# A two-layer attention, retention and convolution network on one core: buffers on multiples of 64 bytes, weights that start some words behind one, a new first phase and split retention values

## The chip, the core and the metric

The kernel runs on one core of one Trainium2 chip. The metric is the device time of one execution in microseconds; before the change it was 2833.11 (median of two runs, 2832.78 and 2833.45). The core has a matrix engine (TensorE, PE in the profile; PEld is its loading of the stationary operand), VectorE (DVE), ScalarE (ACT), GpSimd (POOL) and SyncE (SP, which issues most transfers). The engines run side by side, each through its own list of instructions in order, and wait for each other by semaphores. SBUF is the working memory, 128 partitions wide; a product of TensorE is summed up in a PSUM bank and emptied from there by ScalarE or VectorE.

## The reference

One sequence of 256 tokens, 2048 features, two layers. All weights and activations are float32.

```python
for l in range(DEPTH):                       # 2
    hn = _rmsnorm(h, norm_mix[l])
    if l % 2 == 0:
        h = h + _mixer_ab(hn, ...)           # 8 MoBA heads and 8 NSA heads, 2048 x 5400 in, 2048 x 2048 out
    else:
        h = h + _mixer_c(hn, ...)            # 8 retention heads, 2048 x 12288 in, 4096 x 2048 out
    h = h + _cross_attn(_rmsnorm(h, norm_cross[l]), mem_n, w_q_x[l], w_kv_x[l], w_o_x[l])
    h = h + _conv_ffn(_rmsnorm(h, norm_ffn[l]), w_up[l], conv_w[l], conv_b[l], w_down[l])   # d_ff 5632
return _rmsnorm(h, norm_final)
```

In retention each head has queries and keys of 256, values of 512, and chunks of 128 tokens; in a chunk the output is `(q k^T * decay) v`, and across chunks a decayed state is carried. The values are centred later by a group norm over 512 features.

## The kernel before

Activations are held with features on partitions, in 16 slabs (`xs`, 32 buffers of 512 words): columns 0 to 255 are the activation rounded to float32r (`xhat_hi`, L197, ScalarE), columns 256 to 511 what the rounding left (`xhat_lo`, L200, VectorE). float32r is a 4-byte type that keeps fewer bits of the fraction. Weights come from HBM in pieces of 1024 words a partition (`raw`, 4 buffers) and are split in the same way: `whi` by ScalarE (L232), `wlo` by VectorE (L233), 4 buffers of each, so that splitting can run four pieces ahead of TensorE. Three products, high by high, high by low and low by high, then make one product of almost full float32 precision.

There are two forms. `product_b_steps` has the weights stationary (128 of them at a time) and the slabs moving: L272 sends 512 columns (the high weights against both halves), L277 sends 256 (the low weights against the high half). `product_a_steps` has the activations stationary and the weights moving, 512 wide as a rule, 256 or 280 in the first stage (L307 to L309). One product of the first form takes 32 instructions of L272 and 32 of L277. Attention and retention inside a head use full float32 (L975 to L988 in retention), which TensorE runs in two passes an instruction.

The order on TensorE is the order of the code (`manual_schedule`). Work beside the products, such as a head's attention, stands in generators on a list `side`; after every step of a product `pump` moves the first two on that list forward by one `yield`. So a count of `yield`s fixes how many products lie between two parts of a head. The order on ScalarE and VectorE is set by the framework's scheduler, apart from the first phase, which is written out by hand for ScalarE, VectorE and TensorE.

The first phase (L378 to L414) makes two products at once, the columns 4096 to 4607 of `w_in_ab`, while x and weights come in: it loads `mix` gains, then two slabs of x (L373) and 512 words of both weight pieces (L393) at a time, makes the slab's halves (L197, L200), the weights' halves (L406, L401, L407), and sends the products for two slabs. Its four accumulators are all that there are, so the first `product_a` waits until `halves` (L326, L328) has emptied two of them. `start_steps` (L624) is on `side` then: it loads the rows of x a second time, as tokens on partitions, in eight parts (L376), sums their squares on ScalarE (`norm.add`, L148) and makes the norm's factor `col`, `row` and what hangs on it, the angles of the rotation (`angle_steps`) included.

In retention (`head` in `mixer_c`) the values are scaled by the norm's factor on the way out of PSUM with their sum taken along (L963), then shifted by their mean (L965). `attend` makes `q k^T` (L975, L977), multiplies it by the decay (L979, L980), and two `yield`s later multiplies by the values in float32 (L986, L988).

SBUF buffers lie behind each other, each starting on a multiple of 32 bytes. A few small ones (4 to 128 bytes) come first, and by them all `xs`, `raw`, `whi` and `wlo` buffers start 32 bytes behind a multiple of 64 in the built program.

Of the kernel before, what the change touches and what calls it, by code (L numbers as in the profile page):

```python
# [75 lines left out]
def hybrid_kernel(ctx: ExitStack, tc: tile.TileContext, a, out):  # L76
# [5 lines left out]
    count = [0]  # L82
# [12 lines left out]
    def small(n):  # L95
        return new([P, n], F32, "small", 12)
# [13 lines left out]

    ident = new([P, P])
    make_identity(nc, ident)
    ones = new([P, P])
    pool.memset(ones, 1.0)
# [98 lines left out]


# [150 lines left out]
    SPANS = [range(k, k + 2) for k in range(0, ND, 2)]  # L365
# [5 lines left out]
    def load_x(p):  # L371

        nc.sync.dma_start(x_in[p].rearrange("p s t -> p (s t)"), a["x"][:, 2 * p * S : (2 * p + 2) * S])  # L373
# [5 lines left out]
    with tc.manual_schedule(engines=engines):  # L379
        act.activation(new([P, 1]), eps, AF.Copy, scale=eps)  # L380
        load_par(nc.sync, "mix")
        for p in range(ND // 2):
            i, c = p // 2, slice(p % 2 * 512, p % 2 * 512 + 512)
            if p % 2 == 0:
                raws = [raw_tile() for _ in range(2)]
                his = [new([P, 1024], F32R, "whi", 4) for _ in range(2)]
                los = [new([P, 1024], F32R, "wlo", 4) for _ in range(2)]
            if p < 4:
                load_x(p)
            for q in range(2):  # L390
                if p < 4 or p % 2 == 0:
                    d = c if p < 4 else slice(0, 1024)
                    nc.sync.dma_start(raws[q][:, d], w_ab.part(4 * i, 4, 4096 + 256 * q, 256)[:, d])  # L393
            if p == 3:
                for x in range(4, 8):
                    load_x(x)
            for s in (2 * p, 2 * p + 1):
                xs_mix.append(slab_tile())
                xhat_hi(xs_mix[s], x_in[p][:, s % 2, :], gain("mix")[:, s : s + 1])
            if p == 0:  # L400
                dve.tensor_copy(his[0][:, c], raws[0][:, c])  # L401
            for s in (2 * p, 2 * p + 1):
                xhat_lo(xs_mix[s], x_in[p][:, s % 2, :], gain("mix")[:, s : s + 1])
            for q in range(2):
                if p or q:
                    act.activation(his[q][:, c], raws[q][:, c], AF.Copy)  # L406
# [806 lines left out]
```

## Time and profile before

| | |
|---|---|
| median of two runs | 2833.11 us |
| profiled execution, its own time | 2834.51 us |
| its span, first to last instruction | 2832.8 us |
| TensorE busy | 2812.4 us (99%), 14726 instructions |
| VectorE busy | 1906.3 us (67%) |
| ScalarE busy | 1460.1 us (52%) |
| mean granted TensorE clock | 0.998 |
| transferred | 530.11 MB, 187 GB/s over the span |

The profile gives busy time per engine and per group of instructions with their mean length, what ended the idle time before them, and the chain of work that ended last. A product's length in the groups (391 ns for a 512-wide one) includes its way through the array, which the next product's overlaps; the step from one start to the next, or a stretch of the chain divided by its count, is the time that it costs.

### The profile page before, as it was taken

How to read it: one execution, taken by the hardware profiler on the slowest of the kernel's cores; microseconds unless marked ns; L12 is line 12 of the kernel's file. 1: busy time of each engine (PE TensorE's matmuls, PEld its weight loads, DVE VectorE, ACT ScalarE, POOL GpSimd, SP SyncE). 2: the span in 40 equal slices, each digit the busy share in tenths (PEclk: the TensorE clock that was granted, in tenths of full speed). 3: DMA queues.
4: the chain of work that ended last, by engine and by line, in shares of the span. 5: the costliest groups of instructions: out<-in, count | busy, mean ns of one | idle time of the engine just before them, and what ended most of it. 6: DMA issues, size and time to landing. Idle time of an engine off the chain costs nothing.

```text
span 2832.8 us, 39488 instructions
## 1 busy us (share of the span) xinstructions
PE 2812.4 (99%) x14726; PEld 2406.5 (85%) x14726; DVE 1906.3 (67%) x3147; ACT 1460.1 (52%) x2193; POOL 29.9 (1%) x211
## 2 busy tenths in 40 slices
PE   8999999999999999999999999999999999999998
PEld 7888888888888888888888888888888888888887
DVE  7765776776767677665555555556767767676766
ACT  6454455654545455454444444444665645454544
POOL 0000000000000000000000000000000000000000
PEclk9999999999999999999999999999999999999999
DMA  8535565455555555555555555555545555555554
GB/s 305 171 126 161 180 211 172 170 189 192 187 198 190 189 196 201 194 179 179 179 178 186 193 178 179 182 206 189 189 164 193 186 196 184 193 193 187 197 186 158
DMA packets 150544, 530.11 MB, mean 187 GB/s; under 512 B 17040, under 2 KB 17456, under 8 KB 150352
## 3 DMA queue, kind: packets, MB, share of 16 engines
q1 hardware_dynamic: 148752, 523.65, 54.7%
q0 software_dynamic: 1024, 2.90, 0.3%
q8 instruction: 115, 1.88, 0.3%
q10 hardware_dynamic: 576, 1.05, 0.1%
q14 instruction: 77, 0.63, 0.1%
HBM read 525.43 MB, written 2.10 MB: 186 GB/s over the span
## 4 chain that ended last, share of the span: by engine, by line
PE 98%; DMA 1%; ACT 0%; DVE 0%; SPq 0%; issue 0%; ACTq 0%; DVEq 0%
PE acc L272 32%; PE acc L277 17%; PE acc L307 14%; PE acc L309 14%; PE acc L308 14%; PE bank L350 1%; PE bank L986 0%; DMA t<-in_w_in_ab_dram 0%; PE bank L504 0%; PE bank L496 0%; PE bank L484 0%; DMA t<-in_rows_dram 0%; PE bank L1009 0%; PE bank L589 0%; PE bank L579 0%; PE bank L975 0%
## 5 line engine op out<-in xcount | busy, mean ns | idle before, releaser
L233 DVE TENSOR_TENSOR t<-t,t 128x1024 fp32r<-128x1024 f32 x954 | 1156.6, 1220 | 568.7 <-ACT t L232 522.9
L232 ACT ACTIVATE t<-t 128x1024 fp32r<-128x1024 f32 x954 | 1004.6, 1057 | 739.6 <-PE acc L309 540.6
L272 PE MATMUL acc<-t,t 128*128 128x512 f32 x4096 | 965.9, 391 | 6.2 <-DVE t L200 6.2
L272 PEld LDWEIGHTS acc<-t,t 128*128 128x128 f32 x4096 | 759.7, 188 | 159.1 <-DVE t L200 6.2
L307 PE MATMUL acc<-t,t 128*128 128x512 f32 (+2 forms) x1824 | 713.3, 391 | 4.9 <-DVE t L328 4.9
L309 PE MATMUL acc<-t,t 128*128 128x512 f32 (+2 forms) x1824 | 705.1, 387 | 0.0
L308 PE MATMUL acc<-t,t 128*128 128x512 f32 (+2 forms) x1824 | 704.5, 386 | 0.0
L277 PEld LDWEIGHTS acc<-t,t 128*128 128x128 f32 x4096 | 510.6, 192 | 11.6 <-issue 0.4
L277 PE MATMUL acc<-t,t 128*128 128x256 f32 x4096 | 518.0, 283 | 0.0
L307 PEld LDWEIGHTS acc<-t,t 128*128 128x128 f32 x1824 | 343.9, 189 | 74.7 <-DVE t L328 5.4
L309 PEld LDWEIGHTS acc<-t,t 128*128 128x128 f32 x1824 | 343.6, 188 | 69.5
L308 PEld LDWEIGHTS acc<-t,t 128*128 128x128 f32 x1824 | 343.9, 189 | 68.9 <-issue 1.9
L883 ACT ACTIVATE t<-acc 128x256 f32<-128x256 f32 x176 | 65.8, 374 | 229.6 <-PE acc L272 229.6
L886 DVE TENSOR_TENSOR t<-acc,t 128x256 f32<-128x256 f32 x176 | 74.1, 421 | 157.2 <-ACT t L883 157.2
L889 ACT ACTIVATE t<-t,t 128x256 f32<-128x256 f32 x176 | 103.8, 590 | 1.1
L210 ACT ACTIVATE t<-t 128x256 fp32r<-128x256 f32 x88 | 36.1, 411 | 130.5 <-DVE t L908 130.5
L607 DVE TENSOR_TENSOR t<-t,acc 128x512 f32<-128x512 f32 x148 | 95.1, 680 | 2.8 <-PE acc L1104 2.8
L891 DVE SCALAR_TENSOR_TENSOR t<-t,t,t 128x256 f32<-128x256 f32 x176 | 84.2, 478 | 1.5
L890 DVE SCALAR_TENSOR_TENSOR t<-t,t,t 128x256 f32<-128x256 f32 x176 | 84.2, 478 | 0.2
L326 ACT ACTIVATE t<-acc 128x256 f32<-128x256 f32 x80 | 30.0, 376 | 103.4 <-PE acc L272 103.4
L328 DVE TENSOR_TENSOR t<-acc,t 128x256 f32<-128x256 f32 x80 | 33.4, 419 | 69.7 <-ACT t L326 69.7
L887 DVE TENSOR_TENSOR t<-t,t 128x256 f32<-128x256 f32 x176 | 74.3, 422 | 3.0
(218 smaller groups left out, 1127.6 us busy)
## 6 DMA issues: line engine op xcount, KB each, us to landing
t<-in_w_up_dram SPq DMA_DIRECT2D x352, 512.0 KB, 3.4
t<-in_w_in_c_dram SPq DMA_DIRECT2D x192, 512.0 KB, 3.5
t<-in_w_down_dram SPq DMA_DIRECT2D x176, 512.0 KB, 3.4
t<-in_w_in_ab_dram SPq DMA_DIRECT2D x80, 512.0 KB, 4.2
t<-in_w_out_c_dram SPq DMA_DIRECT2D x64, 512.0 KB, 3.3
t<-in_w_out_ab_dram SPq DMA_DIRECT2D x32, 512.0 KB, 4.2
t<-in_w_kv_x_dram SPq DMA_DIRECT2D x32, 512.0 KB, 3.8
t<-in_w_q_x_dram SPq DMA_DIRECT2D x16, 512.0 KB, 3.2
```

The source lines that it names most:

```text
L232: act.activation(hi[:, 0 : m * ncol], raw[:, 0 : m * ncol], AF.Copy)
L233: dve.tensor_sub(lo[:, 0 : m * ncol], raw[:, 0 : m * ncol], hi[:, 0 : m * ncol].bitcast(F32))
L272: pe.matmul(acc[j], parts[k - k0][0][:, j * P : (j + 1) * P], xs[k], start=(k == 0), stop=(end and k == n - 1))
L277: pe.matmul(acc[j][:, 0:S], parts[k - k0][1][:, j * P : (j + 1) * P], xs[k][:, 0:S], start=False, stop=(end and k == n - 1))
L307: pe.matmul(o, xh, hi, start=(k == 0), stop=False)
L308: pe.matmul(o, xh, lo, start=False, stop=False)
L309: pe.matmul(o, xl, hi, start=False, stop=(k == n - 1))
L607: dve.tensor_add(part(t, g), part(t, g), acc)
L887: dve.tensor_mul(u[:, 2:], t, norm.r)
L889: act.activation(c, u[:, 2:], AF.Identity, bias=cp[:, 3, j : j + 1], scale=cp[:, 2, j : j + 1])
L890: dve.scalar_tensor_tensor(c, u[:, 1 : S + 1], cp[:, 1, j : j + 1], c, op0=ALU.mult, op1=ALU.add)
L891: dve.scalar_tensor_tensor(c, u[:, 0:S], cp[:, 0, j : j + 1], c, op0=ALU.mult, op1=ALU.add)
```

## The change

It has five parts.

1. `new` rounds every two-dimensional tile up to a multiple of 64 bytes a partition, so that every buffer starts on such a multiple; `small` has 10 buffers in place of 12.
2. The halves of the weights get 1040 words in place of 1024 (`part_tile`). Each call of `weights` counts one up (`lots`), and its halves start `lots % 16` words behind the buffer's start. The first phase and the last stage (`finish`) use no shift.
3. The first phase takes slab 0, slab 1 and then pairs; x and weights of each step are loaded in turn; the first two weight pieces go out on ScalarE's queue, and the gains behind the first slab. Eight 128-wide products of a tile of ones, whose result is not used, stand ahead on TensorE; `ones` is filled before `ident`. Weights of slabs 8 to 13 come into free `p` buffers in place of `raw`.
4. `start_steps` loads rows from its second step on and squares them five steps after their load; `angle_steps` is an entry of its own on `side`; `compress` waits for two steps in place of eight; `nsa_group` waits for six steps in place of three before its transposes, and `nsa_head` waits for it.
5. Retention's values and scores are split into float32r halves and multiplied in three products each, in place of one float32 product.

```diff
+        unit = 64 // mybir.dt.size(dt)
+        if len(shape) == 2 and shape[1] % unit:
+            full = [shape[0], -(-shape[1] // unit) * unit]
+            return sb.tile(full, dt, name=name, tag=tag or name, bufs=bufs)[:, 0 : shape[1]]
...
+    def part_tile(tag, shift=0):
+        return new([P, 1040], F32R, tag, 4)[:, shift : shift + 1024]
...
     def weights(w, s0, ns, c0, ncol):
         per = 1024 // ncol
+        lots[0] += 1
+        o = lots[0] % 16
...
-            raw, hi, lo = raw_tile(), new([P, 1024], F32R, "whi", 4), new([P, 1024], F32R, "wlo", 4)
+            raw, hi, lo = raw_tile(), part_tile("whi", o), part_tile("wlo", o)
...
-    SPANS = [range(k, k + 2) for k in range(0, ND, 2)]
+    SPANS = [range(0, 1), range(1, 2)] + [range(k, k + 2) for k in range(2, ND, 2)]
...
+        warm = bank()
+        for _ in range(8):
+            pe.matmul(warm[:, 0:P], ones, ones, start=True, stop=True)
...
+            load_x(ks[0], ks[0] + m)
             for q in range(2):
...
+                (nc.sync if ks[0] else nc.scalar).dma_start(raws[q][:, d], w_ab.part(ks[0] // 4 * 4, 4, 4096 + 256 * q, 256)[:, c])
+            if ks[0] == 0:
+                load_par(nc.sync, "mix")
+                act.activation(new([P, 1]), eps, AF.Copy, scale=eps)
...
-            for i in range(10):
-                if i < 8:
-                    load_rows(*tg[i])
-                if i > 1:
-                    norm.add(*tg[i - 2])
-                if i < 9:
-                    yield
+            for i in range(14):
+                if 0 < i < 9:
+                    load_rows(*tg[i - 1])
+                if i > 5:
+                    norm.add(*tg[i - 6])
+                yield
...
-            yield from angle_steps(0, posi)
...
-            for _ in range(8):
+            for _ in range(2):
                 yield
...
-        side.extend((start_steps(), setup_steps()))
+        side.extend((start_steps(), setup_steps(), angle_steps(0, posi)))
...
-            v = [long(), long()]
+            vh, vl = [[new([P, 512], F32R, *tag) for _ in range(2)] for tag in (("vh", 2), ("long", 9))]
...
+                act.activation(vh[t], v, AF.Identity, bias=sm)
+                dve.scalar_tensor_tensor(vl[t], v, sm, vh[t].bitcast(F32), op0=ALU.add, op1=ALU.subtract)
...
+                ph, pl = new([P, 512], F32R, "p", 7), new([P, 512], F32R, "p", 7)
+                act.activation(ph[:, 0 : S + P], pr[:, 0 : S + P], AF.Copy)
+                dve.tensor_sub(pl[:, 0 : S + P], pr[:, 0 : S + P], ph[:, 0 : S + P].bitcast(F32))
...
-                    pe.matmul(b, pr[:, t * P : (t + 1) * P], v[0], start=True, stop=(t == 0))
-                    if t:
-                        pe.matmul(b, pr[:, S : S + P], v[1], start=False, stop=True)
+                    blocks = [(t * P, 0), (S, 1)][: t + 1]
+                    for c0, i in blocks:
+                        for p_, v_ in ((ph, vh), (ph, vl), (pl, vh)):
+                            pe.matmul(b, p_[:, c0 : c0 + P], v_[i], start=(i == 0 and p_ is ph and v_ is vh),
+                                      stop=(c0 == blocks[-1][0] and p_ is pl))
```

The order on ScalarE at the end of the first phase, before. `t_294` and `t_295` are the last weight pieces of the phase, `t_73` and `t_74` the rows, `t_390` and `t_430` the next product's weights, `acc_111` and `acc_112` the first accumulators.

```order
L406 ACTIVATE t_297<-t_295 128x512
L148 ACTIVATE t_464,t_408<-t_74 128x512
L148 ACTIVATE t_485,t_408<-t_73 128x512
L232 ACTIVATE t_391<-t_390 128x1024
L148 ACTIVATE t_500,t_408<-t_74 128x512
L232 ACTIVATE t_431<-t_430 128x1024
L148 ACTIVATE t_521,t_408<-t_73 128x512
L148 ACTIVATE t_538,t_408<-t_74 128x512
L326 ACTIVATE t_346<-acc_111 128x256
L326 ACTIVATE t_350<-acc_112 128x256
```

And after, where `t_348` is the last weight piece, `t_414` and `t_453` the next product's weights, `acc_117` and `acc_118` the first accumulators.

```order
L423 ACTIVATE t_307<-t_348 128x512
L243 ACTIVATE t_415<-t_414 128x1024
L153 ACTIVATE t_550,t_432<-t_73 128x512
L337 ACTIVATE t_370<-acc_117 128x256
L243 ACTIVATE t_454<-t_453 128x1024
L337 ACTIVATE t_374<-acc_118 128x256
L153 ACTIVATE t_573,t_432<-t_74 128x512
```

Five squares (one more stands ahead of these rows) and two conversions stood between the last weights and the first emptying; now one square and one conversion do.

The order on TensorE where a retention head multiplies by its values, before, between two products of the head's gate (`t_13842` holds the scores, `t_13657` and `t_13658` the values).

```order
L309 MATMUL acc_13818<-t_13864,t_12047 128x512
L986 MATMUL bank_13882<-t_13657,t_13842 128x512
L986 MATMUL bank_13887<-t_13657,t_13842 128x512
L988 MATMUL bank_13887<-t_13658,t_13842 128x512
L307 MATMUL acc_13817<-t_13913,t_12053 128x512
```

And after, where `t_13907` and `t_13908` are the scores' halves, `t_13713` and `t_13714` the values' high halves, `t_13715` and `t_13716` the low ones.

```order
L320 MATMUL acc_13880<-t_13930,t_12071 128x512
L1010 MATMUL bank_13948<-t_13713,t_13907 128x512
L1010 MATMUL bank_13948<-t_13715,t_13907 128x512
L1010 MATMUL bank_13948<-t_13713,t_13908 128x512
L1010 MATMUL bank_13955<-t_13713,t_13907 128x512
L1010 MATMUL bank_13955<-t_13715,t_13907 128x512
L1010 MATMUL bank_13955<-t_13713,t_13908 128x512
L1010 MATMUL bank_13955<-t_13714,t_13907 128x512
L1010 MATMUL bank_13955<-t_13716,t_13907 128x512
L1010 MATMUL bank_13955<-t_13714,t_13908 128x512
L318 MATMUL acc_13879<-t_13985,t_12077 128x512
```

Three float32 products became nine float32r products, at the same place in the gate's product.

More of the change, by code (lines that the diff above doesn't have):

```diff
@@ L81, in hybrid_kernel @@
     ps = ctx.enter_context(tc.tile_pool(name="ps", bufs=1, space=bass.MemoryType.PSUM))
-    count = [0]
+    count, lots = [0], [0]
     def new(shape, dt=F32, tag=None, bufs=1):
@@ L95, in small @@
     def small(n):
-        return new([P, n], F32, "small", 12)
+        return new([P, n], F32, "small", 10)
     def acc_tile():
@@ L108, in slab_tile @@
         return new([P, 2 * S], F32R, "xs", 32)
+    ones = new([P, P])
+    pool.memset(ones, 1.0)
     ident = new([P, P])
     make_identity(nc, ident)
-    ones = new([P, P])
-    pool.memset(ones, 1.0)
     eps = new([P, 1])
@@ L379, in hybrid_kernel @@
     with tc.manual_schedule(engines=engines):
[L380 to L384, printed above, removed]
+        warm = bank()
+        for _ in range(8):
+            pe.matmul(warm[:, 0:P], ones, ones, start=True, stop=True)
+        raws = [None, None]
+        for ks in SPANS:
+            p, m = ks[0] // 2, len(ks)
+            c = slice(ks[0] % 4 * 256, ks[0] % 4 * 256 + 256 * m)
+            if ks[0] % 4 == 0:
+                his = [part_tile("whi") for _ in range(2)]
+                los = [part_tile("wlo") for _ in range(2)]
+            if ks[0] in (0, 4, 14):
                 raws = [raw_tile() for _ in range(2)]
[L386 to L389, printed above, removed]
+            elif ks[0] in (8, 10, 12):
+                raws = [new([P, 512], F32, "p", 7) for _ in range(2)]
+            d = slice(0, 512) if ks[0] in (8, 10, 12) else c
+            load_x(ks[0], ks[0] + m)
             for q in range(2):
[L391 to L397, printed above, removed]
+                (nc.sync if ks[0] else nc.scalar).dma_start(raws[q][:, d], w_ab.part(ks[0] // 4 * 4, 4, 4096 + 256 * q, 256)[:, c])
+            if ks[0] == 0:
+                load_par(nc.sync, "mix")
+                act.activation(new([P, 1]), eps, AF.Copy, scale=eps)
+            for s in ks:
                 xs_mix.append(slab_tile())
@@ L400, in hybrid_kernel @@
             if p == 0:
-                dve.tensor_copy(his[0][:, c], raws[0][:, c])
-            for s in (2 * p, 2 * p + 1):
+                dve.tensor_copy(his[0][:, c], raws[0][:, d])
+            for s in ks:
                 xhat_lo(xs_mix[s], x_in[p][:, s % 2, :], gain("mix")[:, s : s + 1])
@@ L802, in nsa_group @@
             side.extend(nsa_head(g, r, qr[r]) for r in range(4))
-            yield
-            yield
-            yield
+            for _ in range(6):
+                yield
             b = bank()
@@ L810, in nsa_group @@
             dve.tensor_copy(pct, b[:, 0:S])
+            yield
+            yield
             pcts[g] = pct
@@ L822, in nsa_head @@
             yield
-            while len(comp) < 2:
+            while len(comp) < 2 or g not in pcts:
                 yield
```

18 lines of the change are left out of this document (9 added, 9 removed).

## The prediction

> **What bounds the kernel now.** I read the page's busy shares and chain first, to see whether one engine sets the time:
>
> ```profile
> span 2832.8 us, 39488 instructions
> PE 2812.4 (99%) x14726; PEld 2406.5 (85%) x14726; DVE 1906.3 (67%) x3147; ACT 1460.1 (52%) x2193; POOL 29.9 (1%) x211
> PE 98%; DMA 1%; ACT 0%; DVE 0%; SPq 0%; issue 0%; ACTq 0%; DVEq 0%
> ```
>
> TensorE is both busiest and nearly the whole chain. Then the busy time by stretches, to see where it is not busy (columns: stretch, its length, busy time and instructions of each engine, granted clock, DMA share, GB/s):
>
> ```profile
> 0.00:7.00 7.00, 0.80 (x2) 0.71 (x3) 2.09 (x6) 3.12 (x5) 1.15 (x10) 1.00 0.62 197
> 7.00:31.00 24.00, 23.73 (x127) 20.32 (x126) 16.52 (x38) 16.97 (x36) 3.63 (x9) 1.00 1.00 358
> 31.00:36.00 5.00, 0.33 (x1) 0.33 (x2) 2.20 (x4) 4.16 (x10) 0.00 (x0) 0.82 0.97 358
> 250.00:2820.00 2570.00, 2570.00 (x13225) 2198.43 (x13224) 1725.80 (x2686) 1330.94 (x1940) 24.36 (x189) 1.00 0.55 187
> ```
>
> From 250 to 2820 us TensorE never pauses. Apart from the output's tail behind the last product, it pauses in two places only: the first 6.2 us and some 5 us around 33. So an edit pays in three ways: an earlier start, no pause at 33, or fewer nanoseconds per product. For the last I took the chain in order of time, in the first feed-forward stage and in the retention stage (start, length, what):
>
> ```profile
> 577.64 3.83 PE acc L277 x32
> 581.48 7.28 PE acc L272 x32
> ...
> 1509.52 0.86 PE bank L975 x4
> ...
> 1516.32 1.72 PE bank L986 x4
> 1518.04 0.86 PE bank L988 x2
> ```
>
> A 512-wide float32r product takes 7.28/32 = 0.2275 us, a 256-wide one 3.83/32 = 0.1197. The difference over 256 columns is 0.42 ns a column, so 0.2275 − 512 × 0.00042 = 12 ns are fixed, whatever the width. Full float32 goes through in two passes: 256 wide 0.86/4 = 0.215, 512 wide 1.72/4 = 0.430, which is 0.84 ns a column and nothing fixed. So each float32r product carries about 12 ns that the float32 passes do not show. The groups of instructions give their number, and the cost of making the float32r halves of the weights (mean ns behind the comma):
>
> ```profile
> L233 DVE TENSOR_TENSOR t<-t,t 128x1024 fp32r<-128x1024 f32 x954 | 1156.6, 1220 | 568.7 <-ACT t L232 522.9
> L232 ACT ACTIVATE t<-t 128x1024 fp32r<-128x1024 f32 x954 | 1004.6, 1057 | 739.6 <-PE acc L309 540.6
> L272 PE MATMUL acc<-t,t 128*128 128x512 f32 x4096 | 965.9, 391 | 6.2 <-DVE t L200 6.2
> L277 PE MATMUL acc<-t,t 128*128 128x256 f32 x4096 | 518.0, 283 | 0.0
> L307 PE MATMUL acc<-t,t 128*128 128x512 f32 (+2 forms) x1824 | 713.3, 391 | 4.9 <-DVE t L328 4.9
> ```
>
> L308 and L309 have 1824 each as well, and the last stage's L1102 to L1104 have 96: 8192 in `product_b_steps`, 5472 + 96 with activations stationary, 13,760 in all. Twelve ns on each is 165 us, 5.8% of the span. Whether the new addresses touch these 12 ns decides the case; everything else in the diff is worth microseconds.
>
> **The change part by part.** *Start.* Before, the first product waited for two slabs:
>
> ```profile
> 4.29 0.91 ACT L197 ACTIVATE t<-t,t 128x256 fp32r<-128x256 f32 x2 [1.97 <-DMA t<-in_x_dram]
> 4.91 0.43 DVE L401 CAST t<-t 128x512 fp32r<-128x512 f32 x1 [4.91 <-DMA t<-in_w_in_ab_dram]
> 5.67 0.87 DVE L200 SCALAR_TENSOR_TENSOR t<-t,t,t 128x256 fp32r<-128x256 f32 x2
> 6.20 2.08 PE L272 MATMUL acc<-t,t 128*128 128x512 f32 x4 [6.20 <-DVE t L200]
> 8.07 1.06 PE L277 MATMUL acc<-t,t 128*128 128x256 f32 x4
> 8.93 1.72 PE L272 MATMUL acc<-t,t 128*128 128x512 f32 x4
> 10.48 1.11 PE L277 MATMUL acc<-t,t 128*128 128x256 f32 x8
> 1.18 0.42 SPq L373 DMA_DIRECT2D t<-in_x_dram  x1
> 1.65 0.90 SPq L393 DMA_DIRECT2D t<-in_w_in_ab_dram  x2
> ```
>
> A load lands about 3.1 us after its issue (1.18 to 4.29; the first weights 1.65 to 4.91). Now x goes out first on SP, and the first two weight pieces on ACT's queue beside it, so both start where SP's first load stood, near 0.75, and land near 3.7. One `xhat_hi` and one `xhat_lo` (0.91/2 and 0.87/2) make the first product ready at about 4.5: −1.7, between −0.5 (if the table load and two issues hold ACT up) and −2.5. The first eight wide products also ran at (8.07 − 6.20)/4 = 0.47 and (10.48 − 8.93)/4 = 0.39 us in place of 0.23: 4 × 0.24 + 4 × 0.16 = 1.6 us. Eight throwaway products now stand ahead of them in time when TensorE waits anyway, so they cost nothing; without the cover they would be eight 128-wide float32 products, 16 passes of half of 0.215 = 1.7 us. VectorE needs, by an estimate from half the cast (0.43/2), half of 0.87 and two quarters of L233 (1.22/4), at least 1.3 us for each of the first two slabs, and TensorE 4 × (0.2275 + 0.1197) = 1.39; that is close, so I count −1.0, between 0 and −1.6.
>
> *The pause at 33.* Who waited up to 60 us, and the two groups that empty an accumulator:
>
> ```profile
> PE acc L307 <- DVE t L328: 4.9, 1, 4.9
> ACT t L148 <- DMA t<-in_rows_dram: 3.2, 4, 1.4
> ```
>
> ```profile
> L326 ACT ACTIVATE t<-acc 128x256 f32<-128x256 f32 x80 | 30.0, 376 | 103.4 <-PE acc L272 103.4
> L328 DVE TENSOR_TENSOR t<-acc,t 128x256 f32<-128x256 f32 x80 | 33.4, 419 | 69.7 <-ACT t L326 69.7
> ```
>
> `product_a` needs an accumulator that L326/L328 have to empty. On ScalarE the emptying stands behind sums of squares (L148), which wait for their rows to land while the DMA engines are full (0.97 above). After, the squares come five steps later, and between the last conversion of the phase and the first emptying stand one conversion and one square whose rows went out long before. What stays is part of an emptying, 0.38 on ScalarE and 0.42 on VectorE, half of it under the other product: −4.4, between −4.9 and 0. Next late would be `col`, which `start_steps` now sets five steps later: the product that needs it ends two steps on, and a following 11.11 us product (3.83 + 7.28) on the other accumulators covers it. Six steps in place of three in `nsa_group` only give VectorE longer; `angle_steps` moves VectorE work into the same stretch, beside TensorE. Both count nothing; uncovered, a step is a few tenths.
>
> *Retention values.* Six float32 passes of 512 columns a head (1.72 + 0.86 = 2.58 us) become nine float32r products (9 × 0.2275 = 2.05): 0.53 × 8 heads = −4.3. Added are, a head, two ScalarE copies of 512, one of 384 and one VectorE subtraction of 384, each shorter than a 1024-wide conversion (1.06 and 1.22 us), so under 5 us a head on engines that are idle for 1372 and 926 us. The chain from QK to PV grows from two VectorE operations to four steps, with 24 products (24 × 0.2275 = 5.5 us) between; two operations and a conversion waited for on each engine fit in that, so I count nothing; if not, the price is under 1 us × 8.
>
> *Addresses.* In the built program all weight and `xs` buffers stood 32 bytes past a multiple of 64. Now `xs` stands on the multiple; weights start 4 × (n mod 16) bytes behind one, n being the product's count, except in the first phase and the last stage. One place before had another start: 280-wide slices follow each other by 1120 bytes, so each raw's second begins on a multiple of 64 as moving operand (start of six products each, in order):
>
> ```profile
> 49.62 0.29 PE L307 MATMUL acc<-t,t 128*128 128x280 f32 x1
> 50.38 0.29 PE L307 MATMUL acc<-t,t 128*128 128x280 f32 x1
> 51.16 0.29 PE L307 MATMUL acc<-t,t 128*128 128x280 f32 x1
> ```
>
> Six at 32 take 0.76 us, six at 0 take 0.78: 0.127 and 0.130 each, of which 280 × 0.42 = 118 are columns. The fixed part stays at 9 to 12 ns. So the moving start alone does not set it, and I take zero for the addresses. Above, the bound is what these rows cannot resolve, 0.01/6 = 1.7 ns a product. Of the 13,760, 128 of the first phase and 96 of the last stage are not shifted; of the other 13,536, 14 of 16 start elsewhere than at 0 or 32, that is 11,844: × 1.7 ns = +20 us. Below, it is the fixed part itself, which is a rival.
>
> Two rules bear on this. The Trainium skill, page "SBUF — State Buffer", section "Specifications (TRN2)", has SBUF in 16-byte lines and a penalty at each crossing to a new one; this speaks against the shifts, since before every operand began on such a line, and no operand of a float32r product in this trace begins off one. Page "TensorE: Matmul & The Clock Gate" of the Trainium skill, section "Back-to-back issue gap", gives N/2.4 + 2.5 ns, an estimate of 215.8 and 109.2 where the rows above have 227.5 and 119.7; the trace does not agree, and by that rule about 11 ns a product could go, 150 us in the sum.
>
> The writers of the shifted halves are not slowed by odd starts as far as rows show, the next two of the groups:
>
> ```profile
> L891 DVE SCALAR_TENSOR_TENSOR t<-t,t,t 128x256 f32<-128x256 f32 x176 | 84.2, 478 | 1.5
> L890 DVE SCALAR_TENSOR_TENSOR t<-t,t,t 128x256 f32<-128x256 f32 x176 | 84.2, 478 | 0.2
> ```
>
> L890 reads `u` one word later than L891, in the same 478 ns. VectorE has 2832.8 − 1906.3 = 926 us to spare, so L233 would have to grow by 926/954 = 0.97 us before it bound. Zero.
>
> Sum: −1.7 − 1.0 − 4.4 − 4.3 = −11.4 us. The profiled execution took 2834.5 (span 2832.8 and 1.7 around it), 1.4 above the median 2833.1: 2833.1 − 11.4 = 2822. With the bounds, 2833.1 − 13.3 = 2820 to 2833.1 − 4.8 + 20 = 2848 (0.5 of the start and all of the retention remain).
>
> **The rivals.** *The fixed part goes (faster).* Float32r alone has it, and every float32r stationary operand of before began at 32; none on a multiple of 64, so the 280-wide rows cannot clear that side. If it hangs on the stationary start, products with `xs` stationary lose it: 5568 × 12 ns = 67, giving 2755. If it hangs on the moving start after all, `product_b_steps` loses 8192 × 12 = 98, giving 2724; the 280-wide rows speak against it. The Trainium skill's gap rule on the TensorE page, above, has no such fixed part.
>
> *Odd starts cost (slower).* One mechanism, in every shifted product: a start behind the multiple adds another fixed part of the same size. 11,844 × 12 ns = 142 us, giving 2964. It decides the sign from 11.4 us on, 1.0 ns a product, and passes 2% (57 us) from (57 + 11.4)/11,844 = 5.8 ns. For it: no float32r operand of before starts off a multiple of 32. Against: 0 and 32 read alike. The penalty at a line's end that the Trainium skill's SBUF page names, above, would be of this kind; no run here shows it.
>
> *The first phase gains nothing.* DMA is full from 7 to 31 us (1.00 above), so the first phase may wait for the same bytes; then only retention pays, 2829.
>
> **How the numbers follow.** Forecast 0.62; first phase for nothing 0.04; fixed part goes 0.21 (0.13 at 2755, 0.08 at 2724); odd starts cost 0.13, of which 0.03 is a small cost that ends below 2860. The range 2745 to 2860 holds 0.62 + 0.04 + 0.13 + 0.03 = 0.82; the forecast's own is 2820 to 2848. Two per cent is 57 us, about what a measurement of this kernel is taken to tell from no change. Faster by over that (under 2776): 0.21. Slower (over 2890): 0.10. Between: 0.69.
>
> **What would show it.** Start right: the first acc product near 4.5. Pause right: no gap of 4 us near 30. Retention: nine products of 0.23 where six of 0.43 stood. Addresses: rows of 32 at L283/L288 (the new L272/L277) stay at 7.28 and 3.83, whichever n. The prediction is wrong if those lengths move, with n or without; by 1 ns a product it is already 13.8 us.

## The result, and the profile after

The changed kernel takes **2868.9 us** (two runs, 2867.85 and 2869.95) against 2833.11: the ratio is 1.0126 with a 95% interval of 1.0106 to 1.0146. It is slower by 35.8 us, where 11 us less were forecast, and outside the range of 2745 to 2860.

The page of the changed kernel, busy shares and chain:

```profile
span 2868.2 us, 39614 instructions
PE 2853.6 (99%) x14766; PEld 2412.3 (84%) x14766; DVE 1914.9 (67%) x3158; ACT 1478.5 (52%) x2218; POOL 29.9 (1%) x211
PE 99%; DMA 0%; DVE 0%; ACT 0%; issue 0%; SPq 0%
```

TensorE is still the whole chain, and it is busy for 41 us more. The same stretches as before, by engine:

```profile
0.00:7.00 7.00, 5.72 (x25) 5.20 (x26) 2.38 (x7) 3.28 (x6) 1.15 (x10) 1.00 0.65 183
7.00:31.00 24.00, 21.86 (x123) 18.41 (x122) 17.43 (x41) 18.84 (x40) 3.57 (x9) 1.00 1.02 371
31.00:36.00 5.00, 4.16 (x24) 3.95 (x24) 4.86 (x11) 4.28 (x10) 0.00 (x0) 0.73 1.00 366
250.00:2820.00 2570.00, 2570.00 (x13091) 2171.81 (x13090) 1708.36 (x2658) 1329.97 (x1937) 24.43 (x189) 1.00 0.54 185
```

The last row tells most: TensorE never pauses in it, neither before nor now, the granted clock is 1.00 in both, and yet it starts 13,091 instructions in these 2570 us where it started 13,225. No wait was added here. Each product takes longer. The groups of products, and of the conversions that now write to shifted places:

```profile
L244 DVE TENSOR_TENSOR t<-t,t 128x1024 fp32r<-128x1024 f32 x954 | 1157.4, 1221 | 584.6 <-ACT t L243 534.6
L243 ACT ACTIVATE t<-t 128x1024 fp32r<-128x1024 f32 x954 | 1008.8, 1058 | 749.3 <-PE acc L320 540.1
L283 PE MATMUL acc<-t,t 128*128 128x512 f32 x4096 | 984.9, 395 | 0.8 <-DVE t L205 0.8
L288 PE MATMUL acc<-t,t 128*128 128x256 f32 x4096 | 512.9, 282 | 0.6 <-DVE t L424 0.6
L318 PE MATMUL acc<-t,t 128*128 128x512 f32 (+2 forms) x1824 | 718.1, 394 | 1.9 <-DVE t L339 1.9
```

The conversions take 1221 and 1058 ns where they took 1220 and 1057, so writing to odd starts costs nothing. The products of 512 columns went from 391 to 395 and 394 ns, those of 256 from 283 to 282. The chain in order of time, in the same feed-forward stage as in the prediction, shows what that is as a step:

```profile
580.41 3.79 PE acc L288 x32
584.20 7.44 PE acc L283 x32
591.64 3.81 PE acc L288 x32
595.45 7.41 PE acc L283 x32
```

Thirty-two products of 512 columns took 7.28 us each time in this stage; now they take 7.41 to 7.46. Thirty-two of 256 took 3.83 and take 3.77 to 3.83. The two widths go opposite ways.

For the whole program I worked out the mean step from the start of one product to the start of the next from the starts in each trace (ns; "weights stationary" is L272/L283 and L277/L288 behind the first phase, 4032 products each; "activations stationary" is every 512-wide product of L307 to L309 or L318 to L320 and of the last stage, 5375). The rows below the first two belong to the experiments.

| kernel | weights stationary, 512 | weights stationary, 256 | activations stationary, 512 | time, us |
|---|---|---|---|---|
| before | 228.6 | 120.4 | 228.7 | 2833.1 |
| changed | 233.4 | 119.2 | 233.4 | 2868.9 |
| e3, changed, no shift | 232.6 | 118.2 | 232.1 | 2853.3 |
| e6, before, weights 4160 bytes apart | 232.2 | 117.3 | 232.8 | 2856.2 |
| e7, before, slabs 64 bytes on | 230.1 | 117.0 | 234.8 | 2857.7 |
| e9, before, slabs 256 bytes on | 228.6 | 120.4 | 228.7 | 2832.7 |
| e12, before, shift alone | 233.0 | 118.8 | 233.3 | 2868.7 |
| e10, changed, congruent | 228.7 | 120.4 | 228.0 | 2824.8 |
| e13, before, low weights 64 bytes on | 228.6 | 118.3 | 228.7 | 2823.3 |
| e14, changed, congruent, low weights 64 bytes on | 228.7 | 118.2 | 228.0 | 2815.1 |

Before against changed: 4032 × 4.74 ns = +19.1 us, 4032 × −1.26 = −5.1, 5375 × 4.7 = +25.3. That is 39 us. A mean of 228.6 holds steps of 226.7 and a few longer ones after each change of width. (The third column of steps holds those into and out of retention's passes too, which part 5 shortens.)

The start of the changed kernel, ScalarE's and TensorE's rows of the timeline (the changed L202 was L197, L205 was L200):

```profile
3.98 0.51 ACT L202 ACTIVATE t<-t,t 128x256 fp32r<-128x256 f32 x1 [0.73 <-DMA t<-in_par_dram]
4.52 0.48 DVE L205 SCALAR_TENSOR_TENSOR t<-t,t,t 128x256 fp32r<-128x256 f32 x1 [0.67 <-ACT t L202]
5.06 1.14 PE L283 MATMUL acc<-t,t 128*128 128x512 f32 x2 [0.28 <-DVE t L205]
```

And the waits of TensorE up to 60 us that answer to the pause at 33:

```profile
PE acc L318 <- DVE t L339: 1.9, 2, 1.1
```

The first product of a layer starts at 5.06 in place of 6.20, and 4.9 us of pause became two waits of 1.9 together. So the first phase did gain; the products of the other 2800 us lost ten times as much.

### The profile page after: what moved, and what is told of

It is laid out like the page before. It is cut to its first block, busy times and chain, and to the rows that moved or that the text cites. A ratio compares the mean times of both kernels' runs of the same rounds, so it can differ in the third digit from the quotient of the medians.

```text
span 2868.2 us, 39614 instructions
## 1 busy us (share of the span) xinstructions
PE 2853.6 (99%) x14766; PEld 2412.3 (84%) x14766; DVE 1914.9 (67%) x3158; ACT 1478.5 (52%) x2218; POOL 29.9 (1%) x211
## 3 DMA queue, kind: packets, MB, share of 16 engines
q0 software_dynamic: 1024, 2.90, 0.3%
## 4 chain that ended last, share of the span: by engine, by line
PE 99%; DMA 0%; DVE 0%; ACT 0%; issue 0%; SPq 0%
PE acc L283 33%; PE acc L288 17%; PE acc L318 15%; PE acc L319 15%; PE acc L320 15%; PE bank L361 1%; PE bank L1010 1%; PE bank L521 0%; PE bank L513 0%; PE bank L501 0%; DMA t<-in_w_in_ab_dram 0%; PE bank L1032 0%; PE bank L606 0%; PE bank L596 0%; PE bank L993 0%; PE bank L511 0%
## 5 line engine op out<-in xcount | busy, mean ns | idle before, releaser
L244 DVE TENSOR_TENSOR t<-t,t 128x1024 fp32r<-128x1024 f32 x954 | 1157.4, 1221 | 584.6 <-ACT t L243 534.6
L243 ACT ACTIVATE t<-t 128x1024 fp32r<-128x1024 f32 x954 | 1008.8, 1058 | 749.3 <-PE acc L320 540.1
L283 PE MATMUL acc<-t,t 128*128 128x512 f32 x4096 | 984.9, 395 | 0.8 <-DVE t L205 0.8
L283 PEld LDWEIGHTS acc<-t,t 128*128 128x128 f32 x4096 | 758.6, 188 | 170.6 <-ACT t L423 0.9
L318 PE MATMUL acc<-t,t 128*128 128x512 f32 (+2 forms) x1824 | 718.1, 394 | 1.9 <-DVE t L339 1.9
L319 PE MATMUL acc<-t,t 128*128 128x512 f32 (+2 forms) x1824 | 713.3, 391 | 0.0
L320 PE MATMUL acc<-t,t 128*128 128x512 f32 (+2 forms) x1824 | 713.1, 391 | 0.0
L288 PEld LDWEIGHTS acc<-t,t 128*128 128x128 f32 x4096 | 505.3, 188 | 13.9 <-DVE t L424 1.0
L288 PE MATMUL acc<-t,t 128*128 128x256 f32 x4096 | 512.9, 282 | 0.6 <-DVE t L424 0.6
L318 PEld LDWEIGHTS acc<-t,t 128*128 128x128 f32 x1824 | 344.5, 189 | 78.7 <-DVE t L339 2.3
L320 PEld LDWEIGHTS acc<-t,t 128*128 128x128 f32 x1824 | 344.4, 189 | 77.3
```

Source lines behind the costliest of these rows:

```text
L243: act.activation(hi[:, 0 : m * ncol], raw[:, 0 : m * ncol], AF.Copy)
L244: dve.tensor_sub(lo[:, 0 : m * ncol], raw[:, 0 : m * ncol], hi[:, 0 : m * ncol].bitcast(F32))
L283: pe.matmul(acc[j], parts[k - k0][0][:, j * P : (j + 1) * P], xs[k], start=(k == 0), stop=(end and k == n - 1))
L288: pe.matmul(acc[j][:, 0:S], parts[k - k0][1][:, j * P : (j + 1) * P], xs[k][:, 0:S], start=False, stop=(end and k == n - 1))
L318: pe.matmul(o, xh, hi, start=(k == 0), stop=False)
L319: pe.matmul(o, xh, lo, start=False, stop=False)
```

## The experiments

My first theory after the result was that an operand's start modulo 64 bytes decides: in the program of before all float32r operands start at 32, now the slabs start at 0 and the weights anywhere. The expectations call two forms of it A and B, and C or E whatever else it could be. The rival, which became theory D, was that the distance between the operands that follow each other on TensorE decides.

### The starts by themselves (e1, e2)

The first run holds no layer at all, only series of 24 float32r products whose two stationary operands alternate, at every start of 0 to 15 words (a word is 4 bytes) of the moving and the stationary operand:

```diff
+    def series(mo, so, n):
+        b = ps.tile([P, 512], F32, name=f"b{count[0]}", tag="b", bufs=4)
+        for i in range(REP):
+            pe.matmul(b[:, 0:n], st[i % 2][:, so : so + P], mv[:, mo : mo + n], start=(i == 0), stop=(i == REP - 1))
```

> Products alone: no layer is computed; 24 float32r products in a row for every start of the moving operand (0 to 15 words behind a multiple of 64 bytes) by every start of the stationary one (0 to 15), 512 wide, then some 256 wide, then both at other multiples of 64. Theory A (the moving operand's start decides): the 512-wide step is 0.227 us where the moving operand starts 8 words behind a multiple of 64, about 0.2325 at 0, and differs with the start modulo 4 words as in the changed kernel (1: 0.2365, 2: 0.234, 3: 0.2295), all stationary starts alike. Theory B (both operands must start 8 words behind): 0.227 in the one cell 8 by 8, 0.229 to 0.237 elsewhere. Theory C (not the starts): one step in all cells.

Of the 23 steps of a series I take the mean of the last 15, here and in e5. The steps of the 256 pairs of starts lie between 226.7 and 244.8 ns. The four pairs that differ by 32 bytes are 230.1, 231.0, 232.9 and 230.1: no row and no column at 32 stands out, so A and B fell. Two things did show. Moving both operands on by 32 bytes together changes little: the steps for starts of 0 to 7 words and for those of 8 to 15 agree within 2.8 ns in all 64 places, where moving both on by one word changes a step by 3.8 ns on average. And the moving operand's start modulo 4 words counts: the means are 232.7, 236.5, 232.9 and 230.3 ns for 0, 1, 2 and 3 words. Here the two stationary tiles lay 2624 bytes apart, which is 64 modulo 256, and 226.7, the step of the kernel before, came up only in a few single places. When the moving operand was moved on by multiples of 64 bytes, up to 1984, the step stayed at 230 throughout: with the two stationary tiles 64 bytes apart, none of these places gave the short step.

The same question was put to the whole kernel: before, with 32 bytes more in front of everything.

```diff
+    new([P, 8])
```

> The kernel before with one unused buffer of 32 bytes ahead, so that weights and slabs start on multiples of 64 bytes in place of 32 behind one; all else is as before. Theories A and B: 9,568 512-wide products at +5.8 ns and 4,192 256-wide ones at -1.3 ns, +50 us, 2883. Theory C (it was the shifts or another part of the change): 2833, within 3 us.

2832.46, ratio 0.9998 (0.9989 to 1.0007). All operands now start on a multiple of 64 bytes, and nothing happens.

### The changed kernel without its shift (e3, e4)

```diff
-        o = lots[0] % 16
+        o = 0
```

> The changed kernel with every shift at 0. Theories A and B: product_a's mean over the shifts (233.4 ns) becomes that of a start on the multiple (232), product_b's stays: -5 us at most, 2861 to 2869. Theory C with the shifts as cause: 2822 to 2828, the forecast without address costs.

2853.29, ratio 1.0073 (1.0056 to 1.009). This lies between what the theories expected (2861 or more, 2828 or less). The shift costs 2868.9 − 2853.3 = 15.6 us, and 20 of the 36 us are there without it. With 32 bytes more in front, on top of that:

```diff
+    sb.tile([P, 8], F32, name="pad", tag="pad", bufs=1)
```

> The changed kernel with no shift and one unused buffer of 32 bytes ahead, so that every operand of the products starts 32 bytes behind a multiple of 64 as before the change. Theories A and B: steps of 0.2267 and 0.120 again, and only the first phase (4 us) and the retention values (4 us) remain: 2825. Theory C with buffer spacing as cause: 2860 or more.

2853.47, ratio 1.0073 (1.0058 to 1.0088). Starts on or beside a multiple of 64 are out of it a second time.

### The distances (e5)

Again no layer. All three tiles stand at one place modulo 512 bytes; the second stationary operand starts d words behind the first modulo that, the moving operand m words behind the first.

```diff
+        for i in range(REP):
+            c = d * (i % 2)
+            pe.matmul(b[:, 0:n], st[i % 2][:, c : c + P], mv[:, m : m + n], start=(i == 0), stop=(i == REP - 1))
```

> Products alone again, no layer computed; two stationary operands take turns, and what is varied is the distance of the second from the first and of the moving operand from the first, modulo 512 bytes. Theory D (what counts is how far operands lie apart, modulo 256 or 512 bytes, not where they start): 0.2267 us a 512-wide step where both distances are 0, and again at 128 words (512 bytes) or already 64 (256 bytes); 0.229 to 0.237 at distances of 1 to 48 words. Theory E (weights' widths or the number of buffers matter in another way): no cell stands out, as in the run by starts.

Steps in ns, from the starts in the trace, first 512 wide, then 256 wide:

```
512 wide    m=0    m=1    m=4    m=16   m=32   m=48   m=64   m=128 words
d=0        226.7  236.6  231.8  228.9  232.3  233.3  226.7  226.7
d=1        230.1  230.1  230.1  233.3  231.6  232.9  230.1  230.0
d=16       232.7  233.6  233.9  229.9  229.9  230.1  229.6  229.6
d=32       233.3  235.5  229.1  231.7  232.3  230.5  233.3  232.2
d=64       226.7  236.6  231.8  228.9  232.3  233.3  226.7  226.7
256 wide    m=0    m=1    m=4    m=16   m=32   m=48   m=64   m=128 words
d=0        120.0  123.1  113.3  117.8  118.7  113.3  120.0  120.0
d=16       118.2  121.0  118.3  116.5  119.9  117.7  118.2  118.2
```

At d=0 and d=64, distances of 0, 64 and 128 words (0, 256 and 512 bytes) act as one: the pattern has a period of 256 bytes. At distance 0 the 512-wide step is the shortest of all, 226.7, and the 256-wide step is 120.0, among the longer ones. Of single distances up to 64 words, a few others also gave 226.7 (d of 7, 25, 33 and 36 words, m of 7, 15, 39 and 59 among them); I found no rule for these.

Two things limit what the table says. A distance does not always give one step: of the series that were run twice at the same places two settled differently, at 226.7 and 229.9 ns for d=4, m=0, and at 232.7 and 230.2 for d=16, m=0 (which may be why the row d=16 is not the same at m of 0 and 64). And d also changes how far every second stationary operand lies from the moving one. That the two stationary operands count against each other is seen only in that a mixed series is not the mean of its two distances: at d=16, m=16 products at 16 words (228.9 by themselves) and at 0 (226.7) take turns, and the step is 229.9.

In the program of before the slabs are 2048 bytes apart, the halves of the weights 4096, a weight's slices 512 or 1024 or more, and by its small tiles they all start at 288 modulo 512. Every distance was 0 modulo 256, but for 60 of the 280-wide products. After the change the halves are 4160 bytes apart, at eight places modulo 512, and the slabs at 384: of the eight places six are no longer 0 modulo 256 from the slabs, before any shift.

### Breaking one distance in the kernel before (e6, e7, e9)

First the weights' halves 1040 words wide, not shifted:

```diff
-            raw, hi, lo = raw_tile(), new([P, 1024], F32R, "whi", 4), new([P, 1024], F32R, "wlo", 4)
+            raw, hi, lo = raw_tile(), new([P, 1040], F32R, "whi", 4)[:, 0:1024], new([P, 1040], F32R, "wlo", 4)[:, 0:1024]
...
```

(the same in the first phase and the last stage)

> The kernel before with 1040 words in each weights' half and the first 1024 used: the halves lie 4160 bytes apart in place of 4096, starts and all else as before. Theory D: the locked step of 0.2267 is lost as in the changed kernel without shifts, +28 us (its 2853.3 and the 8 us that first phase and retention save): 2861. Theory E or another part of the change as cause: 2833.

2856.23, ratio 1.0084 (1.0069 to 1.0099). Sixteen words that nothing reads or writes cost 23.8 us. This run also holds a comparison within one trace, since a quarter of its products stands at each of four distances of the moving from the stationary operand. At 0, 64, 128 and 192 bytes the mean steps are 229.0, 228.5, 233.1 and 233.3 ns for the 512-wide products of L308 (226.9 before, all at 0), and 121.5, 113.8, 119.8 and 114.2 for the 256-wide ones of L277 (120.4 before).

Then only 64 bytes of padding between the weights' halves and the slabs, so that weights stay congruent with weights and slabs with slabs:

```diff
+            if p == 0:
+                new([P, 16])
```

> The kernel before with one unused buffer of 64 bytes between the weights' halves and the slabs: each group stays a multiple of 512 bytes apart within itself, slabs against weights are 64 bytes off. Theory D in its strict form (all operands): part or all of +28 us, 2845 to 2861. Theory D for each stream by itself (moving against moving, stationary against stationary): 2833.

2857.7, ratio 1.0089 (1.0074 to 1.0104): 25.3 us from one empty tile. And the same with 256 bytes:

```diff
+            if p == 0:
+                new([P, 64])
```

> The program of before with 256 bytes of padding where the run before had 64: the slabs stand 256 bytes further modulo 512 than the weights' halves. Theory D (the distance between operands counts modulo 256 bytes, as the measurement by distances showed): the step stays at 226.7 ns and 120.0, time 2833, ratio 0.998 to 1.002. Rival (the distance counts modulo 512, or any move of the slabs costs): 2857, ratio 1.008 or more.

2832.7, ratio 1.0001 (0.9992 to 1.001). The chain of this run in order of time, at the same place:

```profile
576.99 3.83 PE acc L277 x32
580.83 7.28 PE acc L272 x32
588.11 3.83 PE acc L277 x32
591.94 7.28 PE acc L272 x32
```

And that of the run with 64 bytes:

```profile
572.58 7.32 PE acc L272 x32
579.90 3.77 PE acc L277 x32
583.67 7.33 PE acc L272 x32
591.00 3.63 PE acc L277 x32
```

The same edit with another number makes or takes 25 us. The 3.77 and 3.63 us of the second fence are the same products at the same places: in this run they have two steps, about 118 ns in 68 of the 126 series of 32 behind the first phase and about 113 in 42. In this form of product 7.32 + 3.77 is even less than 7.28 + 3.83; the loss is in the other form, 5375 products with a step of 234.8 in place of 228.7 (+33 us, by the table).

### The shift alone (e12)

The kernel before with halves of 1088 words (4352 bytes, 17 × 256) and the shift:

```diff
+        lots[0] += 1
+        o = lots[0] % 16
...
+            raw, hi, lo = raw_tile(), new([P, 1088], F32R, "whi", 4)[:, o : o + 1024], new([P, 1088], F32R, "wlo", 4)[:, o : o + 1024]
```

> The program of before with the shift alone: halves of 1088 words (4352 bytes, 17 x 256, so that the buffers stay at one place modulo 256 bytes), started product number modulo 16 words behind. Theory D: a shift other than 0 alters the distance to the slabs, so 15 of 16 products lose the short step and pay what the shift costs besides: some 24 x 15/16 + 15.6 = 38 us, 2871, ratio 1.0135. Rival (the shift's cost is its own and the widths' cost another, and the two add up only in the changed kernel): 15.6 alone, 2849, ratio 1.0055.

2868.66, ratio 1.0127 (1.0113 to 1.0141), +36.0 us. So the parts do not add up: the shift costs 36 us where all distances were 0, and 15.6 where they were broken already.

### Mending the changed kernel (e8, e10), and its other parts by themselves (e11)

Without shift and with halves of 1024 words the halves are congruent among each other, but the slabs stood 64 bytes off:

```diff
-        return new([P, 1040], F32R, tag, 4)[:, shift : shift + 1024]
+        return new([P, 1024], F32R, tag, 4)
...
-        o = lots[0] % 16
+        o = 0
```

> The changed kernel without shifts and with 1024 words in each weights' half, so that the halves lie 4096 bytes apart again; the slabs are 64 bytes off against them, modulo 512. Theory D by stream: 2825, the gains of first phase and retention alone. Strict: 2837 to 2853. Theory E: 2853 as without this edit.

2849.65, ratio 1.0062 (1.0045 to 1.0079): hardly better than e3, as e7 says it must be. With 448 bytes of padding in front of the slabs as well, the weights' halves and the slabs all stand at 320 modulo 512:

```diff
+            if ks[0] == 0:
+                new([P, 112])
```

> The changed kernel without shifts, weights' halves of 1024 words, and 448 bytes of padding, so that slabs and weights all start at the same place modulo 512 (at 320, a multiple of 64). New first phase and split retention values stay. Theory D: the steps lock at 226.7 and 120.0 again; what is left is the first phase (some -4 by the two traces: the first product 1.1 us earlier, warm from the start, a shorter pause) and retention (8 heads x (2.58 - 9 x 0.2267) = -4.3): 2833 - 8 = 2825, ratio 0.996 to 0.998. Rival (the new order of the first phase or of retention, not the addresses, lengthens the steps): as without shifts, 2850, ratio 1.006.

2824.81, ratio 0.9971 (0.9961 to 0.9982). The chain in order of time, and the groups:

```profile
576.51 7.28 PE acc L283 x32
583.79 3.83 PE acc L288 x32
```

```profile
L283 PE MATMUL acc<-t,t 128*128 128x512 f32 x4096 | 965.6, 391 | 1.2 <-ACT t L425 0.6
L288 PE MATMUL acc<-t,t 128*128 128x256 f32 x4096 | 518.3, 283 | 0.1
```

The lengths of before are back, 7.28 and 3.83, 391 and 283, with the new first phase and the split retention values in place. The layout of the buffers in the change cost 2868.9 − 2824.8 = 44.1 us; the other parts gave 2832.7 − 2824.8 = 7.9.

Retention alone: the kernel before with the change's part 5, the last pieces of its diff, from `vh, vl` on:

> The program of before with part 5 of the change alone (retention's values and scores split, nine float32r products a head in place of six float32 passes of 512 columns). The prediction's term: 8 x (2.58 - 9 x 0.2275) = -4.3, so 2828.8, ratio 0.9985. These operands do not stand at the same place modulo 256 bytes as each other, so Theory D has 72 products at about 0.232: 8 x (2.58 - 9 x 0.232) = -3.9, 2829.2. If the longer way from scores to values makes TensorE wait: up to 8 x 1 us more, 2833 or above.

2828.83, ratio 0.9987 (0.9978 to 0.9996): −3.9. Its nine products in the chain:

```profile
1512.81 2.08 PE bank L994 x9
```

2.08 in place of 2.58, 8 × 0.50 = 4.0. The interval is too wide to tell 4.3 from 3.9, and the chain has 2.08 where the forecast had 2.05.

### Each width at its own distance (e13, e14, e15)

If each product follows its own distance, the 256-wide products can have another than the 512-wide ones. Only the low weights of the weights-stationary form, the stationary operands of L277, start 16 words on, in buffers of 1088 words:

```diff
+        o = 16 if ncol == 2 * P else 0
...
+            raw, hi, lo = raw_tile(), new([P, 1024], F32R, "whi", 4), new([P, 1088], F32R, "wlo", 4)[:, o : o + 1024]
```

> The program of before, in which only the low weights of the weights-stationary form (the stationary operands of the 256-wide products) start 16 words, 64 bytes, further on, so that the slab lies 192 bytes behind them modulo 256; all else stays at one place modulo 256 bytes. Each product follows its own distance: the 256-wide step goes from 120.4 to about 113.7 (113.3 in the measurement by distances), 4032 x 6.7 ns = -27 us, 2806, ratio 0.9905; the 512-wide stays at 228.6. Rival (neighbours lose the short step too): 117 and 232, 4032 x (-3.4 + 3.4) = 0, 2833 or above.

2823.25, ratio 0.9969 (0.9956 to 0.9981). The chain:

```profile
573.06 3.77 PE acc L278 x32
576.83 7.28 PE acc L273 x32
```

The 512-wide products keep 7.28, the 256-wide ones fall from 3.83 to 3.77: each does follow its own distance. The gain of 9.2 us is a third of the 27 expected. The step became 118.3 and not 113.7; why the series of e5 ran at 113.3 at this distance and the kernel does not, is open. The two accumulators that take turns here, where e5 had one bank, are not the reason, since e6 has them too and its products at 192 bytes step by 114.2; e7 had both steps at one distance. The same on the congruent form of the changed kernel, without the rounding of `new` and with the first activation written to a tile that is there already, which leaves the other operands at 256 modulo 512:

```diff
-        unit = 64 // mybir.dt.size(dt)
...
-        return new([P, 1040], F32R, tag, 4)[:, shift : shift + 1024]
+        return new([P, 1024 if tag == "whi" else 1088], F32R, tag, 4)[:, shift : shift + 1024]
...
-        o = lots[0] % 16
+        o = 16 if ncol == 2 * P else 0
...
-            raw, hi, lo = raw_tile(), part_tile("whi", o), part_tile("wlo", o)
+            raw, hi, lo = raw_tile(), part_tile("whi"), part_tile("wlo", o)
...
-                act.activation(new([P, 1]), eps, AF.Copy, scale=eps)
+                act.activation(stack[:, 0:1], eps, AF.Copy, scale=eps)
```

> The congruent form of the changed kernel (no shifts, without the rounding to 64 bytes, all operands at 256 modulo 512 bytes; new first phase and split retention values stay), with the low weights of the weights-stationary form 64 bytes further on. Each product follows its own distance: 2824.8 - 27 = 2798, ratio 0.9878. Rival: 2825 or above.

2815.11, ratio 0.9939 (0.9926 to 0.9953). And with 60 words in place of 16:

```diff
-        o = 16 if ncol == 2 * P else 0
+        o = 60 if ncol == 2 * P else 0
```

> As the run before, with the low weights 60 words, 240 bytes, further on, so that the slab lies 16 bytes behind them modulo 256, the other distance at which the 256-wide step was 113.3. Each product follows its own distance: 2798 again. Rival: 2825 or above.

2816.65, ratio 0.9944 (0.9932 to 0.9957). Both fall short of the 2798 expected, and both beat the kernel before and the changed one; 2815.1 is 17.3 us below the runs of before beside it (2832.4). That is 0.6%, and the interval is clear of 1.

## Why the prediction was wrong

**What bounds the kernel** was right. TensorE is 99% of the chain, no pause came between 250 and 2820 us, and the price of a product times 13,760 decided the case.

**The step that failed** is "I take zero for the addresses". It is +44 us (changed against e10), 3.2 ns on each of the 13,760 products, where zero was taken and 20 us was the upper bound. Three things in it went wrong.

- The variable. The prediction asked where an operand starts. Whether all start at 0 or at 32 modulo 64 made no difference in e2 and e4; how far they lie from each other modulo 256 bytes makes 24 to 36 us in e6, e7 and e12. The built program showed it: every buffer at 288 modulo 512, in 13,700 of the products. I read that as "32 behind a multiple of 64" and never asked what all of them had in common that the change would end.
- The rows that cleared it. The 280-wide slices do stand at other distances (96 and 192 bytes), and their steps hardly differ: 130.0, 129.5 and 128.4 ns on average at 0, 96 and 192 in the trace of before. But that is a property of this width. At 512 columns nearly every step off distance 0 is longer, at 256 most are shorter, and a width between them told nothing of either. In these rows only the moving operand had moved, too. The bound of 1.7 ns, taken from it, was no bound.
- What was counted. The bound was laid on 11,844 shifted products. The widened buffers alone, with no product shifted, cost 23.8 us in e6, because they take three products in four off distance 0.

The rival "odd starts cost" had the sign, with a chance of 0.13, and the deciding point of 1.0 ns a product, but its mechanism was the start and its price 12 ns. A cost of this kind is there in part: on distances that were broken already the shift still makes 15.6 us (e3), about 1 ns a product; whether by the starts or by the distances that it changes is open. In "the fixed part goes" nothing came true: no layout tried made a 512-wide step shorter than 226.7 in the kernel. The "12 ns that are fixed" were an artefact in part: they came from a line through 0.2275 and 0.1197. The two widths answer to the distance with opposite signs, so through e6's steps of 232.2 and 117.3 the same line leaves 232.2 − 2 × (232.2 − 117.3) = 2.4.

**The start**, −1.7 between −0.5 and −2.5: it became −1.1. The loads were as early as forecast, but the first activation waited 0.73 us for the gains, whose load now stands second on SP's queue (its row is above).

**The cold products**, −1.0 between 0 and −1.6: nothing. From 6.04 us on products step by 0.12 and 0.23 us, where before they did only from 10.5 on. But the phase goes by its loads, 371 GB/s at a DMA share of 1.02 from 7 to 31 us, and TensorE is busy for only 21.9 of these 24 us, where it was for 23.7. That is the rival "the first phase gains nothing", at this one term. The eight throwaway products took 3.78 us and not 1.7; they ended 0.28 us before the first product of a layer and so cost nothing:

```profile
1.00 3.78 PE L394 MATMUL bank<-t 128*128 128x128 f32 x16 [1.00 <-POOL t L117]
```

**The pause at 33**, −4.4 between −4.9 and 0: −3.0 (4.9 to 1.9). Two emptyings wait one behind the other; TensorE's second wait, 0.8 us, was not in the forecast. Together start and pause give −4.1, and the runs say −4.0 (2824.8 of e10 less 2828.8 of e11). That these agree is in part luck. The pause differs from profile to profile (4.9 before and 3.7 in e11; 1.9 changed and 2.4 in e10), and it has a price behind it that the forecast left out. The granted clock, third from the right, falls to 0.5 for a while, in the profile of before and in that of the changed kernel:

```profile
34.20:41.00 6.80, 5.33 (x25) 5.33 (x26) 4.77 (x12) 4.89 (x12) 0.00 (x0) 0.50 0.81 280
33.30:36.70 3.40, 3.40 (x18) 3.40 (x17) 3.23 (x8) 3.29 (x9) 0.00 (x0) 0.50 1.00 373
```

In the first row 25 products of 256 columns take 5.33 us, 0.21 each in place of 0.12, which is some 2.3 us lost. In e10's profile the clock stays at 1.00 from 30 to 41 us.

**Retention**, −4.3: −3.9 in e11. Its longer way from scores to values cost nothing, as forecast.

So the sum of the other terms, −11.4, was −7.9, and with +44.1 that gives 36.2 against the 35.8 measured. The zeros for the conversions, for `col`, `nsa_group` and `angle_steps` held from 250 us on, where TensorE waits for nothing. Ahead of that one new wait stands in the profiles of the changed kernel, e3 and e10, and in neither before nor e11:

```profile
226.38 0.61 PE L501 MATMUL bank<-t,t 128*128 128x128 f32 x3 [1.06 <-DVE t L493]
```

The transposes of a head's softmax wait 1.06 us for VectorE's last step of it. Part 5 alone (e11) does not make this wait, and e10 has it without the shift and the wider halves. That it comes from the new places of the `side` entries (part 4) is likely, but no run shows it.

**What would show it** was named rightly: the rows of 32 at L283 and L288 moved, from 7.28 to 7.41 and more and from 3.83 to 3.79.

On the two rules that the prediction weighed: the page "SBUF — State Buffer" of the Trainium skill, section "Specifications (TRN2)", has a penalty at each crossing to a new 16-byte line, by which a start off a line should pay. In e1 starts one word behind such a line were longer (236.5 against 232.7 ns) and starts three words behind it shorter (230.3), so the trace does not agree with it as a rule. The gap rule on the page "TensorE: Matmul & The Clock Gate", section "Back-to-back issue gap", which that section gives for an isolated product, makes an estimate of 215.8 and 109.2 ns; the shortest steps of any run here were 226.7 and 113.3.

## What to carry to other kernels

Where one engine runs without a pause, ask of a change of layout what all its operands have in common before, not only where each begins: here all distances were multiples of 256 bytes by chance of buffer sizes, and 64 bytes of padding in one place were worth 25 us. Take evidence from the same shape, since another width answered with the other sign or not at all. A row that does not move when one thing is varied clears that thing at that shape, and nothing else.

## What the runs showed of the hardware

- The step of back-to-back float32r products depends on the distance of the moving from the stationary operand, with a period of 256 bytes: 226.7 ns for 512 columns at distance 0, 228.9 to 240 at most others (e5). The distance of one stationary operand from the next seems to count as well (229.9 where 226.7 and 228.9 take turns, e5); no run varies it alone.
- For 256 columns it is the other way: 120.0 at distance 0, 113.3 to 123 elsewhere (e5), and 117.0 to 118.3 in whole kernels (e6, e7, e13). A few odd distances are as short as 0, and one distance can have two steps (113 and 118 ns in e7, 226.7 and 229.9 in e5). What in the chip has this period, the runs do not show.
- Off distance 0 the moving operand's start modulo 16 bytes counts as well: 232.7, 236.5, 232.9 and 230.3 ns at 0, 4, 8 and 12 bytes (e1). The shift walked through all of these, but their mean, 233.1, is only 0.4 above the first; on 5375 products with moving weights that is an estimate of 2 us. The rest of the 15.6 us that the shift costs on broken distances (e3) was not taken apart.
- From the end of a pause of TensorE of 4.9 us on, the granted clock was 0.5 for 6.8 us (before), and with a pause of 3.7 us for 3.4 (e11). Behind two waits of 1.9 us together it was 0.5 for 3.4 us (changed), and with two of 2.4 not at all (e10).
